# Deferring the first normalisation and re-ordering the first loads of an 8-core decoder-layer kernel

## Chip, cores and metric

One Trainium2 chip, one program on its 8 cores (two dies: cores 0 to 3 and 4 to 7). The metric is the device time of the slowest core, in microseconds. Most executions agree within a few tenths of a per cent, but an execution can fall into a slow state: the cores of one die, or of both, show a lower granted TensorE clock and the time is some per cent longer.

"Milestones" below are means over the 8 cores of one profiled run, read from the records of single matmuls. They show differences of 1 us that the slowest core's total, which scatters by several us, cannot show. They are fixed places in PE's program, the same in every kernel: "end of tiles 0 to 3" is the start of the last of their matmuls, "second V tile" begins with the statistic just before it (about 0.5 us ahead of its own first matmul), and "end of the first V quarter" lies ten matmuls, 1.9 us, behind the quarter's last one.

## The reference

One layer, with x of 1118 tokens per core (1024 of a prompt, 64 of samples, 30 of halo) by 2048 channels:

```python
x += 0.5*SwiGLU(rms(x))                       # first FFN: the start is here
h  = rms(x)
x += W_out(sig(gA)*A(h) + sig(gB)*B(h))       # mixer: spatial gating (A), convolution (B)
x += 0.5*SwiGLU(rms(x))
def rms_norm(x, g):                            # per token, over 2048 channels
    return x * rsqrt(mean(x*x) + EPS) * g
def swiglu_ffn(x, w_gu, w_down):
    gate, up = split(x @ w_gu, 2)
    return (silu(gate) * up) @ w_down
```

rms divides each token by one number, so (x*g/rms) @ W = ((x*g) @ W)/rms: the division can be done behind the matmul. The change rests on this.

## The kernel before

Activations lie transposed, channels on the 128 partitions in KC = 16 groups, tokens along the free axis in three segments S1. Weights stream in 1 MB tiles (`gu1`: 44 gate/up tiles) issued by POOL, x is issued by SP. A "unit" (j, s) is gate/up tile j on segment s: 16 gate matmuls and 16 up matmuls into two PSUM banks. The helpers `mm`, `act`, `tt`, `stt`, `ts` and `recip` each add one instruction to one engine's program, in this order, and find their semaphores by themselves. The start:

```python
for si, (c0, n) in enumerate(S1):              # loads: all of x, one after another
    for q in range(4):
        evs.append(P.dma("sp", X1[:, 4*q:4*q+4, c0:c0+n], x_d[:, 4*q:4*q+4, c0:c0+n]))
    xev.append(evs)
W.hold[("gu1", 0)] = xev[0][2:3]               # weight tile i waits for a quarter of segment i
...
for (c0, n) in S1:                             # normalise everything first
    bk = bank()
    for k in range(KC):
        sq = SQB.get()                          # 4 buffers
        act(sq, X1[:, k, c0:c0+n], AF.Square)
        mm(bk, ONESB, sq, k == 0, k == KC-1)    # sum over channels
    finish_stats(bk, c0, n)                     # ACT: sqrt
    invert(c0, n)                               # DVE: reciprocal
    for k in range(KC):
        scale_h(H1, X1, PV_F1, k, c0, n)        # DVE: x * gain * 1/rms -> bf16
def gate_up(nm, i, jj, H, HID, seg):
    ... 32 mm ...
    act(tmp, bg, AF.Silu)
    tt(HID[:, jj], tmp, bu, ALU.mult)
```

At the end of the first FFN the down matmuls run in two passes (768 columns, then 350), and x is spilled to memory (one transfer per channel group) in the second pass, just ahead of the mixer's first weights `w_v`:

```python
P1 = [[(0, 384), (384, 384)], [(768, NT-768)]]
def after_m1(pi, o, m, seg):
    add_square(X1, m, o == 0, *seg)            # running sum of squares for the next norm
    if pi == 1:
        P.dma("sp", xs_d[m], X1[:, m, 0:NM], wk=[("xs", m)])
        ...
```

## Time and profile before

| | before |
|---|---|
| first three runs | 3621.64, 3587.69, 3435.30 us |
| profiled run | 3327.27 us, slowest core 6 with a span of 3325.7 us |
| end of gate/up of tiles 0 to 3 (384 matmuls), mean of the cores | 114.0 us |
| end of the first FFN | 1059.7 us |
| first V tile, second V tile, end of the first V quarter | 1072.4, 1077.9, 1108.0 us |

The page of the profiled run begins so (span; then busy time of each engine, its share of the span, and number of instructions):

```profile
span 3325.7 us, 50664 instructions; the slowest of 8 cores (3317.0 to 3325.7 us)
...
PE 3189.0 (96%) x21149; PEld 1945.7 (59%) x21154; DVE 904.0 (27%) x1660; ACT 471.6 (14%) x910; POOL 179.6 (5%) x304
```

In the rows of this profile a helper's line stands for all its calls; in the kernel before L299 is `mm`, L303 `act`, L313 `ts`, L318 `stt`, L322 `recip`, L923 a DMA. In the changed one they are L300, L304, L314, L319, L323 and L996, and L310 is `tt`. A row of a timeline is start, length, engine, line, operation, output<-input, count, and in brackets the idle time before it and what ended it.

### The profile page before, as it was taken

How to read it: one execution, taken by the hardware profiler on the slowest of the kernel's cores; microseconds unless marked ns; L12 is line 12 of the kernel's file. 1: busy time of each engine (PE TensorE's matmuls, PEld its weight loads, DVE VectorE, ACT ScalarE, POOL GpSimd, SP SyncE). 2: the span in 40 equal slices, each digit the busy share in tenths (PEclk: the TensorE clock that was granted, in tenths of full speed). 3: DMA queues.
4: the chain of work that ended last, by engine and by line, in shares of the span. 5: the costliest groups of instructions: out<-in, count | busy, mean ns of one | idle time of the engine just before them, and what ended most of it. 6: DMA issues, size and time to landing. Idle time of an engine off the chain costs nothing.

```text
span 3325.7 us, 50664 instructions; the slowest of 8 cores (3317.0 to 3325.7 us)
## 1 busy us (share of the span) xinstructions
PE 3189.0 (96%) x21149; PEld 1945.7 (59%) x21154; DVE 904.0 (27%) x1660; ACT 471.6 (14%) x910; POOL 179.6 (5%) x304
## 2 busy tenths in 40 slices
PE   6999999999998999996999999999999999999995
PEld 2666666666664445553666666665666666666653
DVE  4112112112126342223851111136112112112136
ACT  3000000000012122221630000012000000000011
POOL 0000000000000000000420000000000000000000
PEclk9999999999998999998999999999999999999997
DMA  8535435435446977874253444476434334334335
GB/s 181 82 53 85 72 54 86 70 55 86 69 62 121 207 133 157 158 154 87 52 93 66 71 77 77 74 174 102 76 56 91 73 53 86 72 61 90 65 60 158
DMA packets 80432, 307.31 MB, mean 92 GB/s; under 512 B 10000, under 2 KB 32784, under 8 KB 58640
## 3 DMA queue, kind: packets, MB, share of 16 engines
q0 software_dynamic: 36288, 225.53, 40.7%
q1 hardware_dynamic: 43920, 78.54, 8.9%
q8 instruction: 172, 2.82, 0.3%
q14 instruction: 52, 0.43, 0.0%
HBM read 502.77 MB, written 30.19 MB: 160 GB/s over the span
## 4 chain that ended last, share of the span: by engine, by line
PE 88%; DMA 5%; DVE 3%; SPq 1%; issue 1%; ACT 1%; DVEq 0%; ACTq 0%; POOL 0%; POOLq 0%
PE ps L299 88%; DMA gspill<-arena 2%; DVE arena L318 2%; DMA arena<-gspill 2%; SPq L923 1%; ACT arena L303 1%; DMA arena<-xin 1%; DVE arena L309 1%; DMA arena<-cache 0%; DVE arena L322 0%; DMA arena<-w_dn 0%; ACT L303 0%; DVEq L915 0%; ACTq L915 0%; POOL arena L923 0%
## 5 line engine op out<-in xcount | busy, mean ns | idle before, releaser
L299 PE MATMUL ps<-arena 128*128 128x364 bf16 (+11 forms) x21149 | 3189.0, 324 | 128.0 <-DMA arena<-gspill 36.3
L299 PEld LDWEIGHTS ps<-arena 128*128 128x128 bf16 (+2 forms) x21154 | 1945.7, 98 | 1371.0 <-issue 181.1
L309 DVE TENSOR_TENSOR arena<-arena,ps 128x374 bf16<-128x374 f32 (+7 forms) x456 | 223.5, 499 | 1706.8 <-PE ps L299 1706.5
L303 ACT ACTIVATE arena<-ps 128x364 f32<-128x364 f32 (+6 forms) x492 | 237.9, 484 | 2346.4 <-PE ps L299 2346.3
L318 DVE SCALAR_TENSOR_TENSOR arena<-ps,arena 128x364 f32<-128x364 f32 (+8 forms) x467 | 243.1, 526 | 352.2 <-PE ps L299 351.1
L309 DVE TENSOR_TENSOR arena<-arena 128x384 f32<-128x384 f32 (+14 forms) x361 | 229.6, 644 | 187.7 <-ACT arena L303 177.8
L303 ACT ACTIVATE arena<-arena 128x384 f32<-128x384 f32 (+9 forms) x293 | 162.4, 566 | 343.3 <-DVE arena L318 176.4
L318 DVE SCALAR_TENSOR_TENSOR arena<-arena 128x384 bf16<-128x384 f32 (+11 forms) x245 | 133.4, 590 | 3.4 <-ACT arena L303 1.9
L923 POOL DMA_DIRECT2D arena<-w_gu x88 | 46.6, 530 | 1066.5 <-PE ps L299 1007.9
L923 POOL DMA_DIRECT2D arena<-w_dn x73 | 38.5, 528 | 902.5 <-PE ps L299 902.5
L303 ACT ACTIVATE arena<-ps,arena 128x512 bf16<-128x512 f32 (+6 forms) x108 | 53.7, 563 | 121.0 <-PE ps L299 120.9
L309 POOL TENSOR_TENSOR arena<-arena 128x364 f32<-128x364 f32 (+1 forms) x48 | 45.7, 952 | 148.0 <-DVE arena L309 148.0
L322 DVE RECIPROCAL arena<-arena 128x384 f32<-128x384 f32 (+11 forms) x17 | 37.0, 2177 | 47.4 <-ACT arena L303 47.4
L580 DVE BATCH_NORM_STATS2 arena<-arena 128x6 f32<-128x512 bf16 (+1 forms) x36 | 24.8, 692 | 86.7 <-ACT arena L303 86.7
L309 DVE TENSOR_TENSOR arena<-ps,arena 128x384 f32<-128x384 f32 (+1 forms) x48 | 25.4, 530 | 29.1 <-DMA arena<-xspill 15.6
L923 POOL DMA_DIRECT2D arena<-w_gate x16 | 8.6, 534 | 398.0 <-PE ps L299 398.0
L303 ACT ACT_TABLE_LOAD x17 | 21.8, 1283 | 35.2 <-PE ps L299 13.4
L923 POOL DMA_DIRECT2D arena<-w_glu x16 | 8.5, 533 | 273.4 <-PE ps L299 250.3
L923 POOL DMA_DIRECT2D arena<-w_wo x11 | 5.8, 530 | 150.7 <-PE ps L299 150.7
L313 DVE TENSOR_SCALAR arena<-arena 128x2048 bf16<-128x2048 bf16 (+4 forms) x12 | 9.4, 837 | 0.0
L923 POOL DMA_DIRECT2D arena<-cache x16 | 8.9, 557 | 9.6 <-DMA gspill<-arena 9.5
L923 POOL DMA_DIRECT2D arena<-w_v x8 | 4.2, 533 | 94.4 <-PE ps L299 94.4
(10 smaller groups left out, 17.6 us busy)
## 6 DMA issues: line engine op xcount, KB each, us to landing
arena<-w_gu POOLq DMA_DIRECT2D x88, 1024.0 KB, 10.0
arena<-w_dn POOLq DMA_DIRECT2D x73, 704.0 KB, 7.4
arena<-gspill SPq DMA_DIRECT2D x64, 263.0 KB, 6.0
arena<-w_glu POOLq DMA_DIRECT2D x16, 1024.0 KB, 9.9
arena<-w_pab POOLq DMA_DIRECT2D x16, 1024.0 KB, 14.7
arena<-w_gate POOLq DMA_DIRECT2D x16, 1024.0 KB, 10.4
arena<-w_wo POOLq DMA_DIRECT2D x11, 1024.0 KB, 15.1
xspill<-arena SPq DMA_DIRECT2D x16, 544.0 KB, 28.6
```

Source lines behind the costliest of these rows:

```text
L299: return P.op("pe", lambda e: e.matmul(out, lhsT, rhs, start=start, stop=stop), [lhsT, rhs], [out])
L303: return P.op("act", lambda e: e.activation(out=out, in_=in_, func=func, **kw), rd, [out])
L309: return P.op(eng, lambda e: e.tensor_tensor(out=out, in0=in0, in1=in1, op=op), [in0, in1], [out])
L313: return P.op("dve", lambda e: e.tensor_scalar(out=out, in0=in0, scalar1=s1, scalar2=s2, op0=op0, op1=op1), rd, [out])
L318: return P.op("dve", lambda e: e.scalar_tensor_tensor(out=out, in0=in0, scalar=s, in1=in1, op0=op0, op1=op1), rd, [out])
L322: return P.op("dve", lambda e: e.reciprocal(out=out, in_=in_), [in_], [out])
L580: P.op("dve", lambda e, t=t, rows=rows, pr=pr: e.bn_stats(out=ST[0:rows, t, pr, :], in_=V[0:rows, t, pr * 512:(pr + 1) * 512]), [V[0:rows, ...
L923: e.dma_start(out=item[1], in_=item[2]).then_inc(dsem[item[3]], 16)
```

## The change

Intent: let TensorE begin useful matmuls when a third of x and one weight tile are there. Loads alternate (w0, x0, w1, x1, w2, x2, w3; each gated on a quarter or half of the one before), x is contiguous by segment in memory, the first nine units multiply raw activations x*gain and divide by rms when the PSUM banks are read, and the spill leaves by segment. Core of the diff (cuts marked by "..."):

```diff
+        def load_x(si, after=()): ... four quarters of a segment on SP, contiguous
+        def load_w(i, after=()): ... two halves of a tile on POOL
+        w0 = load_w(0)
+        load_x(0)
+        w1 = load_w(1, xev[2:3])
+        load_x(1, w1[0:1])
+        w2 = load_w(2, xev[6:7])
+        load_x(2, w2[0:1])
+        load_w(3, xev[10:11])
...
-        for (c0, n) in S1:            # (normalise everything first: gone)
...
+            stats()                   # in gate_up, behind the unit's 32 matmuls
             tmp = TMPS.get()
+            if defer:
+                up = TMPS.get()
+                tt(tmp[:, 0:n], bg[:, 0:n], RSTD[:, c0:c0 + n], ALU.mult)
+                act(tmp[:, 0:n], tmp[:, 0:n], AF.Silu)
+                tt(up[:, 0:n], bu[:, 0:n], RSTD[:, c0:c0 + n], ALU.mult)
+                tt(HID[:, jj, c0:c0 + n], tmp[:, 0:n], up[:, 0:n], ALU.mult)
+                return
...
-        P1 = [[(0, 384), (384, 384)], [(768, NT - 768)]]
+        P1 = [[S1[0], S1[1]], [S1[2]]]          # 374, 374, 370
         def after_m1(pi, o, m, seg):
             add_square(X1, m, o == 0, *seg)
+            c0, n = seg
+            n = min(n, NM - c0)
+            P.dma("sp", xs_d[m][:, c0:c0 + n], X1[:, m, c0:c0 + n], wk=[("xs", m, S1.index(seg))])
             if pi == 1:
-                P.dma("sp", xs_d[m], X1[:, m, 0:NM], wk=[("xs", m)])
...
+        def head1(run):
+            def start_seg(si, between=lambda: None):
+                c0, n = S1[si]
+                sqs = []
+                for k in range(KC):
+                    sq = SQB.get()               # now 16 buffers
+                    act(sq[:, 0:n], X1[:, k, c0:c0 + n], AF.Square)
+                    ts(H1[:, k, c0:c0 + n], X1[:, k, c0:c0 + n], pv(PV_F1, k), 0.0, ALU.mult, ALU.add)
+                    sqs.append(sq)
+                if si:
+                    rescale(si - 1)              # 16 scale_h of the segment before
+                between()
+                ... stats: 16 mm, sqrt, reciprocal
+                run(0, si, defer=True, stats=stats)
+            start_seg(0)
+            run(1, 0, defer=True)
+            start_seg(1)
+            run(1, 1, defer=True)
+            run(2, 1, defer=True)
+            start_seg(2, lambda: run(2, 0))
+            run(1, 2, defer=True)
+            run(2, 2, defer=True)
+            rescale(2)
+            run(3, 0); run(3, 1); run(3, 2)
```

## The prediction

> **What bounds the kernel now.** I first read the states. The profiled run is a fast one (3327.27 us, all cores at a granted clock of 0.981 to 0.986). The three timed runs, 3435.3, 3587.69 and 3621.64 us, are 3 to 9% above it, so all three lie in the slow state. The mechanisms below are worked out on the fast trace and carried over to the quoted median at the end.
>
> The page gives PE 3189.0 us busy of 3325.7, 96%: the program is TensorE work, 21149 matmuls, and only the 137 us in which PE is idle can be won without removing matmuls. Next I asked for the waits of PE:
>
> ```profile
> PE ps L299 <- DMA arena<-gspill: 36.3, 8, 11.9
> PE ps L299 <- ACT arena L303: 32.3, 12, 9.7
> PE ps L299 <- DVE arena L318: 12.2, 2, 9.7
> ```
>
> The change does not touch the first (the convolution's spill). The second is the start: twelve waits, one for each quarter of x. The stretches of the start (length, busy time of PE, weight loads, DVE, ACT, POOL with counts, then granted clock, DMA share, GB/s) show why:
>
> ```profile
> 0.00:10.00 10.00, 0.29 (x1) 0.13 (x2) 0.32 (x3) 2.34 (x4) 0.20 (x4) 1.00 0.68 165
> 10.00:20.00 10.00, 6.34 (x16) 1.54 (x15) 0.41 (x1) 6.42 (x15) 0.67 (x1) 1.00 1.01 288
> 20.00:30.00 10.00, 2.17 (x6) 0.62 (x6) 9.83 (x16) 2.87 (x7) 0.00 (x0) 1.00 0.99 242
> 30.00:40.00 10.00, 6.24 (x15) 1.46 (x14) 3.14 (x4) 6.22 (x15) 0.53 (x1) 1.00 1.01 241
> 40.00:50.64 10.64, 3.34 (x8) 0.87 (x9) 8.39 (x16) 4.08 (x10) 1.59 (x3) 1.00 0.88 222
> ```
>
> The DMA engines are full from 10 us on while PE has done almost only 48 statistics matmuls. The timeline shows what stands in program order between data and the first useful matmul (start, length, engine):
>
> ```profile
> 16.41 1.73 ACT L303 ACTIVATE arena<-arena 128x374 bf16<-128x374 f32 x4 [0.59 <-DMA arena<-xin]
> 19.59 2.49 DVE L322 RECIPROCAL arena<-arena 128x374 f32<-128x374 f32 x1 [18.10 <-ACT arena L303]
> 22.25 8.39 DVE L318 SCALAR_TENSOR_TENSOR arena<-arena 128x374 bf16<-128x374 f32 x16 [0.17 <-DVE arena L322]
> ...
> 50.64 19.67 PE L299 MATMUL ps<-arena 128*128 128x370 bf16 x108 [0.25 <-ACT arena L303]
> ```
>
> Segment 0 is normalised at 30.6 us, but PE first runs the statistics of all three segments in program order, so the first gate matmul comes after the last x quarter (49.9 us), at about 52.1 us. From there PE has no gap until the end of the first FFN.
>
> **What the skill says.** "DMA: Bandwidth & Descriptors", section "Issuing engines are not separate DMA queues": transfers started by SP and POOL run on the same 16 engines and interleave. The trace agrees: with x on one and weights on the other the DMA share stays at 0.99 to 1.01, it does not add up. So the change can reorder the loads but not widen the pipe. "TensorE: Matmul & The Clock Gate", Part 1: after idling PE runs at half rate until it has been busy for about 3.4 us. The trace agrees: weight loads between 51.8 and 55.2 us come 0.31 us apart, later about 0.155. "ScalarE: Activation LUTs", "What ACT_TABLE_LOAD costs": about 1283 ns for any set; the trace has 17 at a mean of 1283. "VectorE: DVE Perf Modes", "Mode 2×_2P": an fp32 tensor_scalar from SBUF can move two elements a cycle, which a two-tensor op cannot. No row of this trace has that fp32 form.
>
> **The change, part by part.**
>
> 1. *Order of loads.* x is laid out so that each segment is contiguous per partition (runs of about 6 KB instead of 1.5 KB), and weight tiles are issued between segments in halves: w0, x0, w1, x1, w2, x2, w3. Cost of each on the full engines: the SP queue moved 9.51 MB in 55.6% of the first 60 us, 285 GB/s; POOL's weights over the whole page moved 225.53 MB (as bf16; twice that is read) in 40.7% of the span, 333 GB/s of reads. A segment (4 x 748 KiB, 3.06 MB) is 10.7 us, a weight tile (1024 KiB, 2.1 MB read) 6.3 us. With 2 us until the first bytes and 1 us of bubbles in the chain of issues: w0 and x0 are in at about 19 to 20 us, w1 at 26, x1 at 37, w2 at 43, x2 at 54. If longer runs let x move at the weights' 333 GB/s, x1 is in at 34.
>
> 2. *Raw activations first.* H1 is written as x times gain without waiting for the statistics, so gate matmuls need only their own quarter and weights. A gate/up unit is 32 matmuls at 0.155 to 0.158 us, 5.0 us; a segment's statistics are 16 matmuls, 2.5 us dense. Both kernels owe PE 12 units for tiles 0 to 3 (60.5 us); the new one has the 7.5 us of statistics in the stream too, 68. It can do the two units and the statistics of segment 0, and three quarters of a gate of segment 1 (14.5 us together), before x1 is complete. What remains is 53.5 us. All else is available in time: tiles 1 and 2 on segment 1 and tile 2 on segment 0 give 15 us of work after (0,1), up to about 57 us, and x2 is in at 54. End of tile 3: 37 + 53.5 + 1.7 (half clock for 3.4 us) + about 2 for DVE hand-overs = 94 us. Before: 52.1 plus 384 matmuls; the counts of the windows (129 in 20 us) put its end at 113.5. **Gain at the start: 19.5 us.**
>
> 3. *Added work.* Nine deferred units each cost two more DVE operations than before (multiplying both banks by 1/rms; the final product stays), at 0.54 us a row such as the PSUM products, 10 us in all; 48 tensor_scalar writes, 0.35 us by the skill's two elements a cycle plus about 150 cycles (an estimate), at worst the 0.52 of today's scaling, 17 to 25 us; four more table loads, 5 us of ACT. The 48 normalising operations stay as a rescale. DVE in the first 90 us: 29 + 10 + 20 = about 60 us. It fits, but in bursts: after x1, 8.4 us of rescaling and a 2.5 us reciprocal come before the eviction of (0,1), finished at about 50 us. The eight banks hold (0,0), (1,0), (0,1) and two statistics exactly; the first matmul that must reuse a bank of (0,1) is (0,2)'s second at about 57 us. This is why I allow 2 us and no more.
>
> 4. *Boundary of FFN and mixer.* The spill of x now leaves by segment as soon as it is final: two thirds in the first down pass instead of all in the second. In the second pass it collides with the next weights today; core 0 at that boundary:
>
> ```profile
> 1059.78 0.54 POOL L923 DMA_DIRECT2D arena<-w_v  x1 [9.55 <-PE ps L299]
> ...
> 1071.68 13.62 PE L299 MATMUL ps<-arena 128*128 128x512 bf16 x55 [12.44 <-DMA arena<-w_v]
> ```
>
> Issues of w_v take a median 21.9 us to land, against 10.0 for w_gu of the same size; 6.1 of the 8.9 MB of spill goes out of their way. But the 12 us are not all to be had: the second V tile is preceded on PE by the last statistics, which need the last sum of squares, and DVE delivers that at about 1075 us in both (16 steps of 2.7 us). So PE waits there instead: about 2 us won. Against it, V tiles 2 and 5 now straddle a segment boundary (374 and 748 instead of 384 and 768) and need the next segment's scaling one tile (3.5 us) sooner; DVE has it just in time by my count. **Net here: 2 us.** Total columns of the down passes are the same, 1118.
>
> Sum: 19.5 + 2 = 21.5 us, 0.65% of 3326: about 3305 in the fast state.
>
> **Rivals.** (a) *The transfer hides nothing.* DMA was the bound and stays it: if interleaved halves cost the DMA more (x1 at 43 us), only 13 us are won. For: the share is already 1.0, and x gives up bandwidth to the tiles issued before it. Against: before, PE waited for all 9.2 MB of x, now for 3.06 MB and one tile. About 3313. (b) *DVE becomes the bound of the start*: if tensor_scalar costs 0.6 us and the rescales block evictions, banks fill and PE stalls 5 to 8 us: about 3311. (c) *The straddling V tiles* make PE wait 3 to 4 us at the mixer's start: about 3309. (d) *All goes well*: x at 333 GB/s and 8 us of the V wait back: about 3295. None reaches 2% (66 us): all of the start's idle time plus the V wait, 45 and 12 us, is less than that.
>
> **Range and chances.** In the fast state I expect 3305, between 3293 and 3316. The quoted 3587.69 is a median of three slow runs; the gain is a DMA-paced stretch and does not grow with a slower PE clock, so the same state gives 3587.69 - 22 = 3566. The uncertainty of the quoted figure is that of the state: the runs before lie between 3435 and 3622. My range of 3400 to 3615 allows a median in a slow state of any depth; a median of three that falls wholly in the fast state (about 3305) is outside it, and I give that about one chance in ten. Chances, meant for like states: within 2% 0.91, faster 0.07 (mostly from states), slower 0.02.
>
> **What would show it.** Right: first gate matmul before 20 us; PE nearly gapless from about 37 us; tile 3's gate/up finished near 94 us; the DMA share still about 1.0 until 50 us; w_v landing sooner, but a PE wait of several us for DVE before the second V tile. Wrong: PE gaps released by DVE between 40 and 90 us (rival b), x1 landing after 42 us (a), or a change of more than 10 us anywhere after 1200 us, which none of my steps touches.

## More of the kernel before

The prediction shows the start and core 0's boundary of FFN and mixer. One more place turns out to matter: the end of the first FFN on core 6, PE's timeline.

```profile
1049.15 3.42 PE L299 MATMUL ps<-arena 128*128 128x350 bf16 x22 [0.17 <-DMA arena<-w_dn]
1056.38 6.28 PE L299 MATMUL ps<-arena 128*128 128x350 bf16 x22 [3.80 <-DMA arena<-w_dn]
1072.31 37.89 PE L299 MATMUL ps<-arena 128*128 128x512 bf16 x165 [9.66 <-DVE arena L318]
```

The second row is a wait of 3.8 us *inside* the second down pass, for the last down weights, while the spill is on the engines. The third is the start of the mixer.

## The result

Changed kernel: median 3312.60 us (3307.20 to 3910.25, 13 runs); before, with its further runs of the same rounds: median 3435.30 us (3323.53 to 3929.35, 15 runs). A ratio here is the mean time of one kernel's fast runs over that of the other's fast runs of the same rounds, so not quite the ratio of the medians: **0.995, 95% interval 0.9938 to 0.9961**, some 17 us. Of the changed kernel's 13 runs 7 were fast (3307 to 3313 us), of before's 15 also 7 (3324 to 3333), so the one median is the slowest of the fast runs and the other the fastest of the slow ones. The 120 us between the medians are the state, not the change.

The page after (the profiled run is fast; slowest core 5):

```profile
span 3310.8 us, 50847 instructions; the slowest of 8 cores (3294.2 to 3310.8 us)
...
PE 3173.4 (96%) x21154; PEld 1940.2 (59%) x21154; DVE 927.1 (28%) x1724; ACT 477.0 (14%) x914; POOL 183.0 (6%) x308
```

Look at span minus busy PE: 136.7 us idle before, 137.4 after. By this page PE's idle time has not fallen at all, and its *busy* time is down by 15.6 us with the same matmuls. A matmul that is fed late counts as busy for longer (run c5 below shows it), so busy time is not a floor. Over all cores and by stage (mean of 8 cores; length, busy and idle of PE in us; "scatter" means the difference is within what one kernel shows from run to run):

| stage | before: length, busy, idle | after: length, busy, idle | change of length |
|---|---|---|---|
| start, to the end of tiles 0 to 3 | 114.0, 81.8, 32.2 | 96.1, 74.8, 21.3 | -17.9 |
| rest of the first FFN | 945.7, 942.6, 3.1 | 941.2, 941.2, 0.0 | -4.5 |
| to the end of the first V quarter | 48.3, 35.8, 12.5 | 51.3, 37.1, 14.2 | +3.0 |
| the rest of the program | 2212.4 | 2214.6 | +2.2 (scatter) |
| sum (mean span) | 3320.4 | 3303.2 | -17.2 |

So 22.4 us are won by the end of the first FFN and 3 given back at once at the mixer's start. The start on core 5, in the same stretches as the prediction's (length, busy time of PE, weight loads, DVE, ACT, POOL with counts, granted clock, DMA share, GB/s):

```profile
0.00:10.00 10.00, 0.00 (x0) 0.00 (x0) 1.52 (x7) 1.30 (x2) 1.40 (x6) 1.00 0.75 145
10.00:20.00 10.00, 2.84 (x8) 0.93 (x8) 1.57 (x5) 3.45 (x8) 0.00 (x0) 1.00 0.98 257
20.00:30.00 10.00, 8.86 (x42) 4.44 (x43) 2.83 (x8) 3.47 (x8) 1.12 (x2) 1.00 0.73 125
30.00:40.00 10.00, 6.49 (x37) 3.29 (x35) 7.37 (x14) 5.41 (x11) 0.00 (x0) 0.96 0.90 300
40.00:50.00 10.00, 9.99 (x53) 5.03 (x52) 10.00 (x24) 4.96 (x11) 2.25 (x2) 0.86 0.61 94
```

Before, PE had done 40 to 44 of its 48 statistics matmuls by 50 us; now it has begun 140 matmuls. (The trace of this core has its first clock record at 25.6 us, that of core 6 before at 55.3; the clock of 1.00 printed for earlier stretches, in the prediction's table too, is not a reading.) The DMA share no longer stays at 1.0: it falls to 0.73 and 0.61. PE's timeline of the same core:

```profile
14.07 1.40 PE L300 MATMUL ps<-arena 128*128 128x374 bf16 x4 [14.07 <-DMA arena<-w_gu]
16.36 1.44 PE L300 MATMUL ps<-arena 128*128 128x374 bf16 x4 [0.89 <-DVE arena L314]
20.81 1.41 PE L300 MATMUL ps<-arena 128*128 128x374 bf16 x4 [3.01 <-DVE arena L314]
22.55 12.56 PE L300 MATMUL ps<-arena 128*128 128x374 bf16 x68 [0.33 <-DVE arena L314]
38.61 71.70 PE L300 MATMUL ps<-arena 128*128 128x374 bf16 x437 [3.50 <-DVE arena L314]
```

80 matmuls, (0,0), its statistics and (1,0), are done at 35.1 us; then PE stands for 3.50 us until DVE's raw write (L314) of segment 1; from 38.61 there is no gap. What was DVE doing? ACT and DVE from the end of the statistics on:

```profile
30.05 0.57 ACT L304 ACTIVATE arena<-ps,arena 128x374 f32<-128x374 f32 x1 [6.35 <-PE ps L300]
30.73 2.49 DVE L323 RECIPROCAL arena<-arena 128x374 f32<-128x374 f32 x1 [7.36 <-ACT arena L304]
33.33 1.00 DVE L310 TENSOR_TENSOR arena<-ps,arena 128x374 f32<-128x374 f32 x2
33.95 1.28 ACT L304 ACT_TABLE_LOAD   x1 [3.32 <-DVE arena L310]
...
35.87 0.55 DVE L310 TENSOR_TENSOR arena<-arena 128x374 bf16<-128x374 f32 x1 [1.54 <-ACT arena L304]
36.33 1.00 DVE L310 TENSOR_TENSOR arena<-ps,arena 128x374 f32<-128x374 f32 x2
...
38.05 5.32 DVE L314 TENSOR_SCALAR arena<-arena 128x374 bf16<-128x374 f32 x16
```

Square root, reciprocal, the evictions of two units with a table load between, and only then the raw writes: DVE works in program order, and in that order the raw writes of segment 1 stand behind the eviction of (1,0), although that segment's first two quarters had landed at 33.7 and 36.6 us. The chain from the end of the statistics is 8.0 us; PE has 5.05 us of work meanwhile.

The boundary, core 6's PE:

```profile
1048.39 5.31 PE L300 MATMUL ps<-arena 128*128 128x512 bf16 x16 [11.56 <-DMA arena<-w_v]
1056.64 53.66 PE L300 MATMUL ps<-arena 128*128 128x370 f32 x245 [2.94 <-DVE arena L310]
```

The wait for `w_v` is still there (12.5 us as a mean of the cores, 12.7 before), and here the second V tile waits for the last statistics, whose sum of squares (L310) comes from DVE. Six of the eight cores have that wait, of 0.4 to 3.7 us; the mean of all is 1.6. No wait for `w_dn` is left inside the down passes.

### The profile page after: what moved, and what is told of

It is laid out like the page before. It is cut to its first block, busy times and chain, and to the rows that moved or that the text cites. A ratio compares the mean times of both kernels' runs of the same rounds, so it can differ in the third digit from the quotient of the medians.

```text
span 3310.8 us, 50847 instructions; the slowest of 8 cores (3294.2 to 3310.8 us)
## 1 busy us (share of the span) xinstructions
PE 3173.4 (96%) x21154; PEld 1940.2 (59%) x21154; DVE 927.1 (28%) x1724; ACT 477.0 (14%) x914; POOL 183.0 (6%) x308
## 4 chain that ended last, share of the span: by engine, by line
PE 88%; DMA 6%; DVE 3%; issue 1%; ACT 1%; SPq 1%; POOL 0%; DVEq 0%; ACTq 0%; POOLq 0%
PE ps L300 88%; DMA gspill<-arena 2%; DMA arena<-gspill 2%; DVE arena L319 2%; ACT arena L304 1%; SPq L996 1%; DVE arena L310 1%; DMA arena<-xin 1%; DMA arena<-cache 0%; DVE arena L323 0%; DMA arena<-w_gate 0%; ACT L304 0%; POOL arena L310 0%; DVE arena L648 0%; DVE arena L314 0%
## 5 line engine op out<-in xcount | busy, mean ns | idle before, releaser
L300 PE MATMUL ps<-arena 128*128 128x364 bf16 (+10 forms) x21154 | 3173.4, 323 | 127.8 <-DMA arena<-gspill 41.9
L310 DVE TENSOR_TENSOR arena<-arena,ps 128x374 bf16<-128x374 f32 (+7 forms) x448 | 219.2, 499 | 1670.4 <-PE ps L300 1670.1
L319 DVE SCALAR_TENSOR_TENSOR arena<-ps,arena 128x374 f32<-128x374 f32 (+7 forms) x467 | 243.1, 526 | 347.7 <-PE ps L300 346.6
L310 DVE TENSOR_TENSOR arena<-arena 128x364 bf16<-128x364 f32 (+17 forms) x369 | 234.2, 642 | 190.0 <-ACT arena L304 181.7
L304 ACT ACTIVATE arena<-arena 128x364 f32<-128x364 f32 (+11 forms) x301 | 166.2, 566 | 336.8 <-DVE arena L319 175.4
L319 DVE SCALAR_TENSOR_TENSOR arena<-arena 128x374 bf16<-128x374 f32 (+10 forms) x245 | 133.1, 589 | 3.7 <-ACT arena L304 2.3
L996 POOL DMA_DIRECT2D arena<-w_dn x73 | 38.5, 528 | 903.7 <-PE ps L300 891.7
L310 POOL TENSOR_TENSOR arena<-arena 128x364 f32<-128x364 f32 (+1 forms) x48 | 45.7, 953 | 139.7 <-DVE arena L310 139.7
L323 DVE RECIPROCAL arena<-arena 128x374 f32<-128x374 f32 (+10 forms) x17 | 37.0, 2177 | 24.9 <-ACT arena L304 24.9
L310 DVE TENSOR_TENSOR arena<-ps,arena 128x384 f32<-128x384 f32 (+3 forms) x64 | 33.5, 533 | 29.1 <-PE ps L300 15.3
L314 DVE TENSOR_SCALAR arena<-arena 128x374 bf16<-128x374 f32 (+6 forms) x60 | 25.6, 498 | 16.9 <-DMA arena<-xin 16.3
L996 POOL DMA_DIRECT2D arena<-w_pab x16 | 8.7, 544 | 6.6 <-PE ps L300 6.6
(10 smaller groups left out, 17.4 us busy)
## 6 DMA issues: line engine op xcount, KB each, us to landing
arena<-w_pab POOLq DMA_DIRECT2D x16, 1024.0 KB, 12.5
```

Source lines behind the costliest of these rows:

```text
L300: return P.op("pe", lambda e: e.matmul(out, lhsT, rhs, start=start, stop=stop), [lhsT, rhs], [out])
L304: return P.op("act", lambda e: e.activation(out=out, in_=in_, func=func, **kw), rd, [out])
L310: return P.op(eng, lambda e: e.tensor_tensor(out=out, in0=in0, in1=in1, op=op), [in0, in1], [out])
L314: return P.op("dve", lambda e: e.tensor_scalar(out=out, in0=in0, scalar1=s1, scalar2=s2, op0=op0, op1=op1), rd, [out])
L319: return P.op("dve", lambda e: e.scalar_tensor_tensor(out=out, in0=in0, scalar=s, in1=in1, op0=op0, op1=op1), rd, [out])
L323: return P.op("dve", lambda e: e.reciprocal(out=out, in_=in_), [in_], [out])
```

## The experiments

All edits are to the changed kernel, and every kernel gave correct results. They ran in five rounds on five different chips, each with the kernel before beside it; the changed kernel, run again in the fourth round, repeats its milestones within 0.4 us. Milestones (us, means of the cores of the profiled run; all profiled runs fast, except that one die of c3's was slow and its row is cores 0 to 3). "Restart" is the first matmul of segment 1, "gap" PE's idle time just before it.

| run | x1 landed | restart | gap | end of tiles 0-3 | FFN end | 2nd V tile | V quarter end | ratio to before, 95% |
|---|---|---|---|---|---|---|---|---|
| before | 34.4 | - | - | 114.0 | 1059.7 | 1077.9 | 1108.0 | 1 |
| changed | 40.1 | 37.9 | 3.5 | 96.1 | 1037.4 | 1057.6 | 1088.6 | 0.995 [0.9938, 0.9961] |
| changed, again | 40.1 | 38.1 | 3.5 | 96.3 | 1037.8 | 1057.7 | 1088.4 | 0.9986 [0.993, 1.0042] |
| a1 | 39.5 | - | - | 127.3 | 1068.7 | 1088.8 | 1119.6 | 1.0022 [0.997, 1.0074] |
| a2 | 30.9 | - | - | 110.0 | 1051.3 | 1071.5 | 1102.2 | 0.997 [0.9926, 1.0015] |
| a3 | 42.0 | 39.0 | 3.4 | 97.4 | 1038.7 | 1058.9 | 1089.8 | none given |
| a4 | - | - | - | 96.5 | 1039.3 | 1060.5 | 1091.8 | 0.9944 [0.9892, 0.9997] |
| b1 | 39.2 | 41.7 | 3.6 | 99.9 | 1041.2 | 1061.5 | 1092.6 | 0.9944 [0.9901, 0.9987] |
| b2 | 40.0 | 38.0 | 3.4 | 96.3 | 1037.5 | 1057.7 | 1088.3 | 0.9932 [0.9903, 0.996] |
| b3 | - | - | - | 96.4 | 1037.8 | 1057.5 | 1088.9 | 0.9942 [0.9899, 0.9985] |
| b4 | 40.1 | 38.5 | 3.6 | 96.3 | 1037.6 | 1058.4 | 1088.9 | 0.9941 [0.9899, 0.9984] |
| c1 | 40.0 | 36.3 | 1.6 | 97.7 | 1039.0 | 1059.3 | 1090.4 | none given |
| c2 | 36.8 | 44.1 | 1.9 | 102.2 | 1043.5 | 1063.6 | 1094.2 | 0.996 [0.9945, 0.9975] |
| c3 | 37.3 | 42.7 | 0.0 | 98.3 | 1039.5 | 1059.7 | 1090.0 | 0.9953 [0.9939, 0.9967] |
| c4 | 37.1 | 42.4 | 0.0 | 98.2 | 1039.7 | 1059.8 | 1090.5 | 0.9949 [0.9934, 0.9964] |
| c5 | 40.2 | 36.7 | 1.8 | 97.0 | 1038.3 | 1058.6 | 1089.7 | 0.996 [0.9946, 0.9975] |
| d1 | 40.5 | 36.2 | 1.6 | 97.4 | 1038.6 | 1057.5 | 1088.8 | 0.994 [0.9927, 0.9954] |
| e1 | 40.4 | 39.8 | 3.8 | 102.5 | 1044.0 | 1064.0 | 1094.8 | 0.9957 [0.9937, 0.9976] |
| e3 | 40.2 | 37.9 | 3.3 | 96.3 | 1037.9 | 1057.9 | 1089.2 | 0.9938 [0.9924, 0.9953] |

### The two halves of the change: a1 and a2

a1 keeps the new loads but normalises each segment before its first matmul; a2 keeps the deferral but takes the old order of loads.

```diff
 # a1
-                    ts(H1[...], X1[...], pv(PV_F1, k), 0.0, ALU.mult, ALU.add)
+                bk = bank(); ... 16 mm; finish_stats; invert; rescale(si); run(0, si)   # per segment
-            run(1, 0, defer=True)
+            run(1, 0)
 # a2
-        w0 = load_w(0); load_x(0); w1 = load_w(1, xev[2:3]); ...
+        load_x(0); load_x(1); load_x(2)
+        load_w(0, xev[2:3]); load_w(1, xev[6:7]); load_w(2, xev[10:11]); load_w(3)
```

> The changed kernel with the old arithmetic: statistics, reciprocal and scaling come before each segment's gate/up again, the new loads, layout and early spill stay. Milestone: end of the gate/up units of tiles 0 to 3 (114.0 us before, 96.1 us after, mean of 8 cores). Theory 1 (both parts are needed: the reordered loads only pay if PE need not wait for the 11 us chain of square root, reciprocal and sixteen scalings after each segment): milestone near 107 us, fast time 8 to 12 us above the changed kernel's 3310. Rival (the load order alone carries the gain): milestone within 2 us of 96, time within 3 us of the changed kernel.

> The changed kernel with the old order of issues: x0, x1, x2 one after another on SP, weight tiles 0, 1, 2 released by the third quarter of x0, x1, x2; deferred normalisation and contiguous x stay. Theory 1: tile 1 lands only at about 45 us and tile 2 near 58 us as before, so PE waits for weights instead of x; milestone 101 to 106 us, 5 to 10 us above the changed kernel. Rival (deferral alone carries the gain): milestone within 2 us of 96.

Each half alone is poor: the loads alone end the tiles 13.3 us *later* than before, the deferral alone 4.0 sooner, both 17.9 sooner. Both missed what was expected of them (107 and 101 to 106, measured 127.3 and 110.0), to the side that says that both parts are needed. a1, core 5, PE's waits up to 115 us (line waited for, total, times, longest) and two rows of its timeline:

```profile
PE ps L300 <- ACT arena L304: 16.7, 3, 10.0
PE ps L300 <- DVE arena L319: 15.1, 3, 5.4
```

```profile
54.77 29.49 PE L300 MATMUL ps<-arena 128*128 128x374 bf16 x144 [5.40 <-DVE arena L319]
...
89.63 25.65 PE L300 MATMUL ps<-arena 128*128 128x370 bf16 x123 [5.37 <-DVE arena L319]
```

Three waits of 4.4 to 5.4 us for the first scaled group, once a segment, and behind each a unit at DVE's 0.52 us a step. Before, the loads of later segments hid that chain. a2, core 3: PE waits for weights, which now stand behind x:

```profile
PE ps L300 <- DMA arena<-w_gu: 33.6, 4, 25.3
PE ps L300 <- DVE arena L314: 1.9, 1, 1.9
```

What follows: early data is worth nothing while the statistics stand in the path, and a free path is worth little while the weights come last.

### Contiguous x and the early spill: a3 and a4

```diff
 # a3: the old layout of x (runs of 1.5 KB instead of 6 KB), loads and order as changed
-    x_d = din("xin", [128, KC * NT])
+    x_d = din("xin", [128, KC, NT])
 # a4: the spill by segment, but all of it in the second pass
             if pi == 1:
+                for si, (c0, n) in enumerate(S1):
+                    P.dma("sp", xs_d[m][:, c0:c0 + n], ...)
```

> The changed kernel with x in DRAM in the old layout, so the loads read 1.5 KB runs again (SBUF layout and everything else unchanged). If long runs matter to the rate, x1 lands 2 to 4 us later than 40.0 us (mean of the cores) and the milestone moves from 96 to 98 to 100 us. If the rate is set elsewhere, both stay within 1 us.

> The changed kernel with the whole spill of x back in the second down pass (three pieces per row block). Theory: the start is untouched (milestone 96), the weight waits of the second down pass come back (about 3 us of PE waits for w_dn), and the first FFN ends 3 to 4.5 us later than 1037.4 us; but the second V tile, which waits for the last sum of squares, starts at 1057.6 plus at most 2 us, so the total changes by 0 to 3 us. Rival (the spill is what delays the V weights and the total): V starts 8 us or more later than 1049.9 and the total is 6 us or more longer.

a3: x1 lands 1.9 us later and the tiles end 1.3 later; the total shows nothing. a4: the FFN's end (counted from the end of the tiles) comes 1.5 us later, the first V tile at 1054.5 instead of 1049.9, the V quarter 3.2 later; at the end of the profiled run 0.5 us of it is left in the mean span (3303.7 against 3303.2), over the undisturbed dies of all its runs 2.5 (3304.9 against 3302.4), near the scatter. The early spill works in two places. *Inside* the down pass, waits for `w_dn` are back in a4, but only 1.0 us of them as a mean, where 3 were expected. And `w_v` lands later: from the first issue to the landing of its second tile it is 22.8 us in a4, as before the change, and 18.6 in the changed kernel.

### The gap in the DMA share: b1

The share of 0.73 at 20 to 30 us is a bubble: w1 waits for x0's third quarter and starts late. b1 gates each weight tile one quarter sooner.

```diff
-        w1 = load_w(1, xev[2:3])
+        w1 = load_w(1, xev[1:2])               # and w2, w3 likewise
```

> The changed kernel, but each weight tile is released by the second instead of the third quarter of the x segment ahead of it. In the changed kernel the DMA engines idle for about 3 us (20 to 24 us) before x1, between the landing that releases tile 1 and its first bytes. Theory: this bubble is what made x1 land at 40.0 us instead of the predicted 37; here it closes, x1 lands at 37 to 38 and the milestone (end of gate/up of tiles 0 to 3) moves from 96.1 to 93 to 94.5 us. Rival (the rate is the limit, bubbles are only gaps between landings): both stay within 1 us.

A miss, and instructive. x1 landed 0.9 us sooner, w1 1.3 sooner, yet the tiles end 3.8 us *later*. b1's PE on core 3:

```profile
25.38 13.90 PE L300 MATMUL ps<-arena 128*128 128x374 bf16 x68 [4.03 <-DVE arena L314]
42.86 57.46 PE L300 MATMUL ps<-arena 128*128 128x374 bf16 x345 [3.58 <-DVE arena L314]
```

w1 took its bandwidth from x0, whose last quarter landed at 24.3 us instead of 21.3 (means), and the restart followed it, by 3.8 us for these 3.0, with the same gap of 3.58 us. So in the changed kernel the restart hangs on x0's last quarter plus a chain of 16.6 us, 17.4 in b1 (the rest of (0,0), the statistics, the 8.0 us shown above), not on x1's landing.

### Moving DVE's order, and the gate of x1: c1 to c4

c1 puts the raw writes of segment 1 ahead of the eviction of (1,0); c2 lets x1 go without waiting for w1; c3 does both; c4 also does the statistics of a segment between the gate and the up matmuls.

```diff
 # c1
+            raw(1)                              # ts of segment 1, taken out of start_seg(1)
             run(1, 0, defer=True)
 # c2
-        load_x(1, w1[0:1])
+        load_x(1)
```

> The changed kernel, but on DVE the sixteen raw writes of segment 1 come before the eviction of unit (1,0) instead of behind it; loads unchanged. New theory after the gates run: PE resumes on segment 1 not when x1 lands but a fixed 16.6 us after x0's last quarter (statistics, square root, reciprocal, two evictions, then the raw writes), after a gap of 3.5 us in every core, and needs 58.1 us from there. Here the gap of 3.5 us before the 81st matmul shrinks to the wait for x1's quarters, matmuls 81 to 92 are then paced by x1 (last quarter at 40.0), and the milestone moves from 96.1 to 93 to 95 us. Rival (x1's landing is the bound): milestone stays within 0.7 us of 96.1.

> The changed kernel, but x1 is queued right behind x0 instead of waiting for the first half of weight tile 1; the order on DVE is unchanged. x1 should be in 2 to 4 us sooner (36 to 38 us), weight tile 1 some 3 us later. New theory: no gain, since the raw writes still stand behind the eviction of (1,0), which itself comes later with tile 1: milestone 96 to 98.5 us. Old reading (x1's landing sets the milestone): 92.5 to 94 us.

> Both edits: raw writes of segment 1 before the eviction of (1,0), x1 queued right behind x0. If the two bounds stand one behind the other, the pair gives more than the sum of its parts: no PE gap before the 81st matmul, milestone 91 to 93 us, total 3 to 5 us below the changed kernel. If one alone is the bound, the better of the two single runs is not beaten by more than 0.5 us.

> The pair of edits, and the statistics matmuls of a deferred unit run between its gate and its up half instead of after both, so the chain of square root and reciprocal starts 2.5 us (16 matmuls) sooner. If DVE's chain behind x0 is still on the path, the milestone gains up to 2.5 us against the pair; if x1 and weight tile 1 are now the bound, it stays within 0.7 us.

c1 has the restart 1.6 us sooner and half the gap, and ends 1.6 us *later*. ACT's rows of core 1 show where the wait went:

```profile
34.00 0.52 ACT L304 ACTIVATE arena<-arena 128x374 f32<-128x374 f32 x1
40.91 7.00 ACT L304 ACTIVATE arena<-arena 128x374 f32<-128x374 f32 x17 [6.39 <-DVE arena L310]
```

The squares of segment 1 stand behind the silu of (1,0) in ACT's order, that waits for DVE's eviction (L310), and the eviction now stands behind the raw writes. ACT sits idle for 6.39 us, and the 16 statistics matmuls of segment 1, done in 2.7 us in the changed kernel, take 4.7 at the pace of ACT's squares. c2 has x1 3.3 us sooner, but w1 6.9 us later (36.0 against 29.1), and (1,0) needs w1. c3 and c4 remove the gap altogether and still end at 98.2 to 98.3, where 91 to 93 was expected of c3: core 1 of c4,

```profile
31.58 1.43 PE L300 MATMUL ps<-arena 128*128 128x374 bf16 x8 [1.80 <-DMA arena<-w_gu]
36.74 63.47 PE L300 MATMUL ps<-arena 128*128 128x374 bf16 x384 [3.74 <-DMA arena<-w_gu]
```

has PE waiting for w1 instead. The early statistics (c4 against c3) are worth 0.1 us.

### Both engines' order out of the way: c5

```diff
+            raw(1)                              # ts AND squares of segment 1
             run(1, 0, defer=True)
```

> Both the raw writes (DVE) and the squares (ACT) of segment 1 stand ahead of the eviction of (1,0), loads as in the changed kernel. My present theory (program order of DVE and ACT paces the restart in the changed kernel, x1's landing is only a little behind it): the restart comes at 36 to 37 us as in the run with raw writes alone, the statistics matmuls of segment 1 no longer stall (2.6 us for the last quarter instead of 4.7), x1's last quarter (40 us) sets the pace from there, and the end of tiles 0 to 3 falls to 94 to 95.5 us (changed kernel 96.1, raw writes alone 97.7). Rival (half clock): the early restart is again fed in pieces, runs at half clock for several us and ends at 97 or later. Time: within 0.1% of the changed kernel's ratio (0.995) either way.

The squares no longer stall (statistics of segment 1: 2.7 us). PE reaches the last quarter of segment 1 at 41.1 us, 0.8 sooner than in the changed kernel (41.9) and just behind x1's landing at 40.2. So x1's landing and DVE's order bound the changed kernel within 0.8 us of each other. Yet the tiles end at 97.0. Segment 2's first unit shows why; the changed kernel's core 5, then c5's, from 60 to 70 us (columns as above):

```profile
60.00:70.00 10.00, 10.00 (x66) 6.10 (x64) 9.74 (x26) 7.16 (x18) 2.25 (x4) 1.00 0.85 169
```

```profile
60.00:70.00 10.00, 9.95 (x55) 5.05 (x53) 9.74 (x26) 7.30 (x18) 0.00 (x0) 1.00 1.07 187
```

and DVE of c5 there:

```profile
61.50 5.24 DVE L314 TENSOR_SCALAR arena<-arena 128x370 bf16<-128x370 f32 x16
```

At full clock PE does 55 matmuls in place of 66: ten of them run 0.32 us apart, DVE's pace of 5.24/16 = 0.33. PE arrived a little earlier and the raw writes of segment 2 no sooner (61.50 against 60.93 in the changed kernel), since they stand in DVE's order behind the evictions and the rescaling of the segments before (DVE was 97% busy over those 10 us). The same gate matmuls of (0,2) take 3.8 us instead of 2.5 as a mean of the cores. Of the 1.7 us that c5 loses behind 41.1 us this is 1.3; the other 0.4 are lost in the units before, on the three cores (1, 2 and 4) whose clock fell to a half there. My theory's 94 to 95.5 missed; the rival named the right number, but mostly for the wrong reason.

### Why weights start late: e1

POOL's two issues of a weight tile took 4.21 us on core 1 of the changed kernel. DVE at that time, and POOL:

```profile
38.17 5.29 DVE L314 TENSOR_SCALAR arena<-arena 128x374 bf16<-128x374 f32 x16
```

```profile
39.89 4.21 POOL L996 DMA_DIRECT2D arena<-w_gu  x2 [18.59 <-DMA arena<-xin]
```

The first of the two took 3.68 us and ended at 43.57 us, 0.12 us after the last of the 16 tensor_scalars (43.45); on core 4 it took 3.87 and ended 0.12 us after them. Meanwhile (core 1, stretches of 2 us):

```profile
40.00:42.00 2.00, 1.99 (x8) 0.68 (x7) 2.00 (x7) 2.00 (x7) 2.00 (x1) 0.50 0.04 13
42.00:44.00 2.00, 2.00 (x9) 0.77 (x9) 2.00 (x7) 2.00 (x6) 2.00 (x2) 0.67 0.00 0
```

nothing moves. The Trainium skill, "SBUF — State Buffer", section "Who interferes with whom", has a rule that fits: DVE in a mode with two ports and GpSimd take the same port pair exclusively, tensor_scalar can enter that mode, and a DMA issued by POOL needs GpSimd to write its descriptors. e1 takes the mode away: the raw writes that can meet an issue become an operation of two tensors, with ones as the second.

```diff
+            memset(SS[:, 0:374], 1.0)
-                    ts(H1[...], X1[...], pv(PV_F1, k), 0.0, ALU.mult, ALU.add)
+                    if si == 1 or (si == 0 and k >= 8):
+                        stt(H1[...], X1[...], pv(PV_F1, k), SS[:, 0:n], ALU.mult, ALU.mult)
+                    else: ts(...)
```

> The raw writes that can meet an issue of weights by POOL (second half of segment 0, all of segment 1) become a scalar_tensor_tensor with a tensor of ones, the same result bit for bit, which has no two-elements-a-cycle form. Lock theory (POOL cannot write its descriptors while back-to-back tensor_scalars hold the port pair that both share): in the changed kernel's profile POOL's first issue of tile 2 took 3.68 us on core 1 and 3.87 on core 4 and ended 0.11 to 0.12 us after the last tensor_scalar; here every such issue takes 0.53 to 0.7 us on all eight cores, and from that issue to x2's last landing it is 18.5 to 20.5 us on all cores, not 22.5 to 22.8 on three. Rival (the memory side is busy and POOL's stretch is chance): holds of over 1 us on one to three cores again. Both: the restart is paced by DVE at 0.52 us a step instead of 0.33, so the end of tiles 0 to 3 comes 1 to 3 us later than 96.1; x1's landing stays at 40 (its gate was not held on any core), and the time within 0.2% of the changed kernel.

```profile
40.05 1.06 POOL L1001 DMA_DIRECT2D arena<-w_gu  x2 [18.91 <-DMA arena<-xin]
```

That is core 1 again (L1001 is the same DMA helper). On all eight cores each issue took 0.53 to 0.54 us, and from the issue of tile 2 to x2's last landing it was 18.7 to 20.7 us, against 22.5 to 22.8 on the three cores that were held. That no issue was held in e1 would not be enough, for six runs with the fast write, b4 among them, have no hold of over 2 us either. The ends are: the runs here other than before and e1 hold 20 issues of over 2 us, and all 20 ended 0.12 us after a train of tensor_scalars did. So the lock is shown. It is rare: 441 issues fell into such trains, where each write begins before the last has ended, and most were not held (b4, core 5: 0.53 us); what decides which are stays open. It costs x2 about 3 us where it strikes, and nothing of the time, for x2's raw writes start later anyway. The second half missed: I expected 1 to 3 us for DVE's slower writes and it was 6.4 (102.5 against 96.1; mean span of undisturbed dies 3308.8 against 3302.4). So the fast form of tensor_scalar carries more of the gain than its 3 us a segment suggest: PE follows those writes at 0.52 us a step where it followed at 0.33, and its clock stays at half for longer (10.7 us as a mean, 3.4 in the changed kernel).

### The boundary: b2, b3, b4, d1, e3

b2 issues the second pass's spill only behind the first V tiles. b3 lets DVE scale between a square and its sum, so that it is not behind with the last sum. b4 cuts segments at 384 and 768, so that no V tile of 128 tokens straddles a boundary. e3 is b2 with b3; d1 is e3 with c5.

```diff
 # b2
-            P.dma("sp", xs_d[m][...], X1[...], ...)
+            if pi == 0: spill()
+            else: late.append(spill)            # run behind the first V tiles
 # b3
-            add_square(X1, m, o == 0, *seg)
+            add_square(X1, m, o == 0, *seg, between=lambda: pops(pi, o))
 # b4
-S1 = [(0, 374), (374, 374), (748, 370)]
+S1 = [(0, 384), (384, 384), (768, 350)]
```

> The changed kernel, but the last segment's spill (2.8 MB) waits until the first quarter of V is done, so nothing but weights loads at the boundary. Theory (two waits one behind the other): the first V matmul comes 5 to 8 us sooner than 1049.9 us, but the second V tile stays at 1057.6 within 1.5 us, because the last sum of squares on DVE sets it; total within 2 us of the changed kernel. Rival (V weights alone bound the boundary): second V tile and total 5 us sooner.

> The changed kernel, but in the second down pass DVE does the two pending scalings while ACT squares, instead of waiting 0.7 us for the square first. Sixteen steps of 2.74 us become about 2.2 us, so the last sum of squares is ready about 8 us sooner. If DVE alone set the second V tile, it would start 7 to 8 us sooner than 1057.6; theory (V weights land at 1050 and stand behind it): only 1 to 3 us sooner, total 1 to 3 us shorter.

> The changed kernel with segments 384, 384, 350 instead of 374, 374, 370, so no V tile straddles a segment. Tests the prediction's worry about straddling: from the second to the last V tile of the first quarter it took 30.1 us before and 31.0 after; here 30.1 again. Start: segments 0 and 1 are 2.7% larger, milestone 96 to 97.5. Total within 1.5 us of the changed kernel.

> The same, plus the two boundary edits (the second pass's spill issued after the V stage's first tiles, and the scaling between square and sum on DVE). If the parts add, the first V quarter ends 1 to 2 us before the changed kernel's 1088.6, and the time is 1 to 4 us below the changed kernel's; if each wait is replaced by the next one, first V quarter at 1088 to 1090 and no difference.

> The changed kernel with the two boundary edits alone (last spill later, scaling between square and sum), its start untouched. Run singly each was replaced by the other's wait. If they add up: end of tiles 0 to 3 at 96.1 to 96.5, second V tile 1.0 to 1.5 us sooner than 1057.6, first V quarter near 1087.3, time 1 to 2 us below the changed kernel's (ratio 0.9945 within 0.001). If w_v's landing is what remains: first V tile at 1050, second at 1057.5, no difference.

b2: the first V tile is at 1050.4 (changed: 1049.9), where 5 to 8 us less were expected, so the second pass's spill is not what `w_v` waits for once the rest has gone early. b3: the second V tile does not move (1057.5; 1 to 3 us were expected), since the first now comes at 1051.7. e3 does not add them up; core 1:

```profile
1052.35 23.08 PE L300 MATMUL ps<-arena 128*128 128x512 bf16 x96 [14.99 <-DMA arena<-w_v]
```

As a mean of the cores the wait ahead of the first V tile is 14.2 us (12.5 in the changed kernel), and from the first to the second it is 5.8 us (7.7): a longer wait for `w_v` has taken the place of the one for DVE. b4: the stretch from the second V tile to the end of the quarter is 30.5 us, against 31.0 with straddling tiles and 30.1 before. But the other straddling kernels on fast cores have 30.2 to 31.3 there, so a cost of the straddle is not shown; it is at most about 1 us.

### Scatter: the changed kernel again

> The changed kernel itself, unedited, as a control for scatter. Both theories: end of tiles 0 to 3 at 96.1 us within 0.5, first V quarter at 1088.6 within 1, and the stretch from there to the end, 2214.6 us in the profiled run, within 2 us; ratio 0.995 within 0.0015. If the stretch differs by more than 2 us from itself, no variant of mine can be told from the changed kernel by its total.

The milestones repeat within 0.4 us. From the first V quarter to the end it is 2214.3 us against 2214.6; over all kernels here, which are alike in that stretch, 2210.1 to 2216.4. The ratio's wide interval comes from a run of 3348 us, counted as fast, with two cores at a clock of 0.971.

Does any version beat the changed kernel? b2, e3 and d1 have the lowest ratios, 0.9932, 0.9938 and 0.994, its own is 0.995; the intervals overlap widely, the first V quarter ends no sooner in e3 and d1 and 0.3 us sooner in b2, and the rest of their gains lies in the stretch that scatters. None is shown to be faster. Apart from a1 and the control's disturbed ratio, those with a ratio lie 0.3 to 0.7% below before.

## Why the prediction was right or wrong

**The quoted time was wrong by its last step, the state.** The prediction carried 21.5 us over to a slow median and said "the same state gives 3587.69 - 22 = 3566", with "about one chance in ten" for a fast median. That step failed: the measured median, 3312.60 us, is a fast run. Three slow runs out of three were too few to hold to, the more so as the one profiled run was fast: over all 173 timed runs 103 were fast (39 of 66 of the kernel before). Near one half, a median of several runs falls in either state about as often, and the range should have held both, or the fast state should have been the centre. The fast-state figure: predicted 3305 (3293 to 3316), measured 3307 to 3313 in the fast runs, -21.5 us against some -17.

**"Only the 137 us in which PE is idle can be won" was wrong.** Of the 17.2 us of the mean span 7.1 came out of busy time (3180.9 to 3173.8), 10 out of idle time (139.5 to 129.5). The prediction had the evidence: 6.34 us for 16 statistics matmuls in one stretch, next to its own "2.5 us dense" (fed slowly or at a half clock: there is no clock record there).

**Start: mechanism right, 19.5 predicted, 17.9 measured.** In the terms of its sum "37 + 53.5 + 1.7 + 2 = 94", the changed kernel has 37.9 + 54.7 + 3.5 + 0 = 96.1:

- *Restart.* 37.9 was hit, for the wrong reason. x1 lands at 40.1, not 37 (37.9 to 38.9 on cores 0, 2, 4 and 6, 41.2 to 41.9 on the others), and PE restarts before that, released by DVE's order, on a fixed time after x0 (b1). The landing bounds it 0.8 us behind that (c5).
- *Work left.* "three quarters of a gate of segment 1 ... before x1 is complete" happened in part: when x1 was complete PE had begun 2 to 12 of these 12 matmuls, 7 as a mean. The step held that a gate matmul needs "only its own quarter and weights", and left out the in-order engine that writes it. At the restart all 352 matmuls remain, 54.7 us at 0.1555.
- *Half clock.* 1.7 was too small, because in the first quarters PE also follows DVE's 0.33 us a step (the first 16 matmuls took 5.2 us, not 2.5); together 3.5 us.
- *Hand-overs.* The 2 us allowed for full banks were not needed: 0.1 us of gaps between restart and the end of the tiles.
- *DMA share.* "still about 1.0 until 50 us" was wrong: 0.73 and 0.61 in two stretches. The bubbles of the gates are wider than the 1 us allowed, and DVE's own raw writes can lock POOL out (e1). The section of the skill that says so was not looked up.

**Added work.** tensor_scalar at 0.35 us was near (16 in 5.32 us, 0.33 each): "VectorE: DVE Perf Modes", "Mode 2×_2P", has fp32 tensor_scalar at twice the rate of a two-tensor operation, which took 0.52 here.

**Boundary: 2 predicted, 1.5 measured.** Counted from the end of the tiles, the first V tile came 4.6 us sooner than before, the second 2.4 and the end of the quarter 1.5. What the prediction did say came true: `w_v` landed sooner (18.6 us from its first issue, not 22.8), and PE waits for DVE ahead of the second V tile. What it did not have: PE's own wait for `w_v` stayed (12.5 us, before 12.7). The early spill also took 3.1 us of w_dn waits out of the down pass (the prediction read PE there as having "no gap until the end of the first FFN"), so the FFN's end, where PE begins to wait, came 6.4 us after that issue, not 10.5. The straddle, "just in time", costs at most about 1 us, not the 3 to 4 of rival (c).

**Rivals.** (a) x1 at 43: no, 40.1. (b) DVE as the bound: half right. It bounds the restart and the raw writes of segment 2, and with a slower write (e1) the loss is 6.4 us, much what (b) gave for 0.6 us. No stall by full banks was seen. (d) did not come.

**What stays open.** Why `w_v` takes 18.6 us from its issue on, and 18.9 in b2, where the second pass's spill is gone too; which issues the lock catches; why one core of a pair gets its weights sooner (below); and how much of the -17 us a better order could add, since every edit met another gate within 2 us.

## What to carry to other kernels

When a chain of engines is tuned close, a start has several gates within a microsecond or two (here a landing, DVE's order, ACT's order, the next tile's landing): taking one away shows the next one, so list for each gate what stands second before putting a number on it. A load that is ready is of use only from the moment the in-order engine that converts it gets to it, so read that engine's program order as closely as the DMA share. Never carry a median of three runs over where there are two states: predict the fast state and give the other its own probability.

## What the Trainium skill lacked or had wrong

- "SBUF — State Buffer", "Who interferes with whom": right, and the prediction should have used it: POOL was held for 3.68 and 3.87 us and freed 0.12 us after DVE's last tensor_scalar. It speaks of one instruction; here the hold ran on through 10 and more back to back (0.325 us apart, each 0.41 long), while on cores 3 and 7 an issue that came 0.01 us behind the end of a write, before the next had begun, took 0.54 us. Nor does it say how seldom that is: 20 holds of over 2 us among 441 issues inside such trains. It calls it inferred that tensor_tensor doesn't hold up descriptors; e1's scalar_tensor_tensor agrees (0.53 to 0.54 us on all cores).
- "HBM Reference", "Specifications (TRN2)" has the two cores of a pair share a memory, each getting about half. Here the halves were not even from moment to moment: in ten of the thirteen runs with this order and these gates of the first loads, exactly one core of each pair (0,1), (2,3), (4,5), (6,7) got the first half of w1 sooner by about 1 us or more, in the changed kernel in 5.1 to 5.6 us against 6.9 to 7.5, with x1 about 3 us apart. Which of the two it was changed from run to run. That these pairs are the page's, and why one is ahead, was not tested.
- "TensorE: Matmul & The Clock Gate", Part 1, agrees after a true gap: behind 3.5 us of idling the granted clock was 0.50 at 40 to 42 us (core 1). But core 1 of c5 fell to 0.50 at 42 to 46 us with no gap above 1.9 us, while its matmuls came in pieces of eight and four. The page does say that frequent short idles can bring the half rate too ("A second HAM failure mode"), but gives no length for them.
- "Perfetto Trace Analysis", "Identifying the Most-Contended Engine", calls matmul busy time a bad measure because pipelined matmuls look smaller in a trace. It does not say that busy time can also hold the waits between matmuls that are fed one by one: core 5 of c5 showed 9.95 us busy for 55 matmuls between 60 and 70 us, the changed kernel 10.00 for 66, both at a granted clock of 1.00.
